# Turning the attention probabilities: one path for all query groups, a common column layout for the scores, and a later schedule

## The chip, the cores and the metric

The kernel runs on one core of a Trainium2 chip. The metric is the time of one execution in device microseconds; the median of three runs is given, and beside it one execution that the hardware profiler recorded. The core has five engines, each with its own queue of instructions that it works through in order: TensorE (PE, matrix products; its weight loads are shown as PEld), VectorE (DVE), ScalarE (ACT), GpSimd (POOL), and SyncE (SP), which here issues the weight transfers. Engines wait for one another through semaphores. Products are accumulated in PSUM, a memory of its own, which the kernel hands out in slots.

## The reference

A sequence of 256 tokens of width 2048 goes through two layers in float32. The first is a Mamba-2 mixer. The second is sliding-window attention with 32 query heads in 4 groups; each group of 8 heads shares one key/value head of width 64. The window is 128, and each head has a sink that enters the softmax's denominator. Cut to the attention part:

```python
proj = x @ w_in
q    = rope(proj[..., :2048] + q_bias)        # (b, s, 4 groups, 8 heads, 64)
gate = proj[..., 2048:]
s = einsum("bcqhrd,bckhd->bchrqk", q_blocks, k_prev_and_own) * 64 ** -0.5
s = where((0 <= q - k) & (q - k < 128) & (k >= 0), s, -inf)
m = maximum(max(s), sink)
p = exp(s - m);  p = p / (sum(p) + exp(sink - m))
o = einsum("bchrqk,bckhd->bcqhrd", p, v_prev_and_own)
h = (o * silu(gate)) @ w_out
x = layernorm(ALPHA * x + h)
```

The 256 queries are two halves of 128 (`h` in the kernel). The first half sees only its own 128 keys under a causal mask. In the second half each query sees the last 128 keys, so a block of 64 queries touches 192 key columns: 64 that are cut by the window's far edge, 64 that are seen in full, and 64 that are cut by the diagonal.

## The kernel before

All large products are done to float32 accuracy with three matmuls: ACT copies the rounded high part of a weight (`wh`, L163), DVE subtracts to get the low part (`wl`, L166), and PE adds high·high, high·low and low·high. Weights come in units of 128x2048, as two transfers of 512 KB each on SP's queue (L154) into six raw buffers; the split runs two units ahead of the products.

The Mamba layer, its output and the shared keys and values fill about the first 685 us. Then comes the attention layer, whose stream of products is written out in `B_ORDER`: for each of the four groups `j` a query projection `q`, a gate projection `g` and an output projection `o`, four weight units each. After every unit `tick()` runs the small jobs whose count has come down to zero; `later(n, fn)` books a job `n` units ahead. The small jobs stand in the engines' queues at the place where they are run, apart from a scheduler that may move DVE, ACT and POOL instructions that are not pinned with `keep_in_program_order`. The jobs of one group are:

- `q_block`: four units of products (L975), then DVE adds the bias and rotates the first 16 columns of each head (rope, L957 to L965). One unit later `qtr` turns the queries: PE transposes (L1061), ACT copies them out of PSUM with the scale (L1065).
- `attend(j, 0)`, two units after the projection, and `attend(j, 1)`, three units after that (one for the last group): PE computes the scores (L1114 for the first half, L1121 for the second). For the second half the two blocks of 64 queries have their 192 columns at different places of the tile, and DVE selects the masked pieces with copies under a predicate on 64 rows each (L1137), after ACT copied the 128 columns in the middle (L1134). DVE takes the maximum (L1145), ACT the exponentials (L1151), DVE normalises (L1157).
- Turning the probabilities, so that keys lie on partitions. For all but one case this is `turn_far`: DVE turns 32x32 blocks (L1170), ACT moves the blocks of 32x256 to their places (L1179: 10 copies for the first half, 16 for the second), and for the second half DVE then multiplies two full copies with masks (L1186, 128x1024). The last group's second half uses `turn_p`: eight PE transposes (L1199) and four DVE multiplications by masks out of PSUM (L1205).
- `pv`: PE multiplies by the values (L1231 for the first half; L1245 and L1252 for the second), DVE multiplies by the gate out of PSUM into `o` (L1219), and ACT and DVE split the result (L1259, L1260) for the output projection. `o` shares its two buffers (tag `qt`) with the rotated queries. The PVs of both halves stand next to one another.
- `o` units: products L322 to L324, added to the residual stream by DVE (L329).

The scores, the query and key transposes, `turn_p` and the PVs share one pool of four PSUM slots (`ax`); the projections use another of four (`mm`). Beside all this the first layer's normalised rows get their gain and offset (`residual`, L1028 and L1029) in eight pieces spread over units 2 to 15, with the gain and offset rows fetched by four pairs of transfers on POOL's queue (`load_affine`, L1023) as the buffers come free. The keys are turned by `ktr` (L1012), two units after their projection, after a copy on POOL (L1007).

Of the kernel before, what the change touches and what calls it, by code (L numbers as in the profile page):

```python
# [83 lines left out]
def trunk(ctx: ExitStack, tc: tile.TileContext, A: dict, out: bass.AP, dbg=None):  # L84
# [31 lines left out]

    tri, anti = cc[:, 256:384], cc[:, 640:768]
    mask_a0 = cc[:, 768:896]
# [137 lines left out]

    def later(n, fn):
        pending.append([n, fn])

# [693 lines left out]
    def rope(v, h, n):  # L953

        c = cs[:, h : h + 1, :].to_broadcast([P, n, 8])
        s = sn[:, h : h + 1, :].to_broadcast([P, n, 8])
        t = bp.tile([P, 4, 8, 8], F32, tag="rt", name=nm("rt"), bufs=1)  # L957
        x1, x2 = v[:, :, 0:8], v[:, :, 8:16]
        a, b, d, e = [t[:, i, :n, :] for i in range(4)]
        nc.vector.tensor_tensor(a, x1, c, ALU.mult)  # L960
        nc.vector.tensor_tensor(b, x2, s, ALU.mult)
        nc.vector.tensor_tensor(d, x2, c, ALU.mult)
        nc.vector.tensor_tensor(e, x1, s, ALU.mult)
        nc.vector.tensor_tensor(x1, a, b, ALU.subtract)
        nc.vector.tensor_tensor(x2, d, e, ALU.add)  # L965

    def x_stat(ps, h, u, ui, pin=False, last=None):
# [3 lines left out]
        for k, i in todo:  # L971
# [7 lines left out]
            pinned(m, pin)  # L979


    kT = bp.tile([P, 4, S], F32, tag="kT", name="kT")
# [3 lines left out]
    for h in range(2):  # L986
        ps = mm_tile()
        for ui in range(4):
            if h == 0:

                kv_u.append(next_unit(ui == 1))
                if ui == 0:
                    center(1, *scale1)
            x_stat(ps, h, kv_u[ui], ui, h == 0, ((1, 1, 2, None), (1, None, None, None))[h][ui])
            if h == 0:
                for c in ((), (), (0, 1, 2, 3), ())[ui]:
                    if c % 2 == 0:
                        wide = bp.tile([P, 1024], F32, tag=("pt0", "pri")[c // 2], name=nm("x1"), bufs=1)
                    turn_x1(1, c, wide[:, c % 2 * 512 : c % 2 * 512 + 512])
        kd = bp.tile([P, 4, 2, 64], F32, tag="qt", name=nm("kd"), bufs=2)  # L1000
        nc.vector.tensor_tensor(
# [14 lines left out]

        later(2, ktr)

    def load_affine(c):

        for i, n in enumerate(("lng", "lnb")):
            gb1[i] = bp.tile([P, 512], F32, tag=f"gb{i}", name=nm("gb1"), bufs=1)
            nc.gpsimd.dma_start(gb1[i][:], A[n][0, c * 512 : (c + 1) * 512].partition_broadcast(P))  # L1023

    def residual(c, h):

        v = xr[:, h, c * 512 : (c + 1) * 512]
        tc.keep_in_program_order(nc.vector.tensor_tensor(v, v, gb1[0][:], ALU.mult))  # L1028
        nc.vector.tensor_tensor(v, v, gb1[1][:], ALU.add)  # L1029

    gb1 = {}
    load_affine(0)
    for c in range(4):
        if c:
            later(GB_AT[c], lambda c=c: load_affine(c))
        for h in range(2):
            later(RES_AT[2 * c + h], lambda c=c, h=h: residual(c, h))

    qT = {}
    sg = {}  # L1040
    os_ = {}
    firsts = []

    def q_block(j):
# [7 lines left out]
        for h in range(2):  # L1052
# [16 lines left out]

            later(1, qtr)  # L1070

# [13 lines left out]

    def first_pt():

        if not firsts:
            t = bp.tile([P, 4, 8, 32], F32, tag="pt0", name="pt0", bufs=1)
            for c in range(1, 4):  # L1090
                nc.gpsimd.memset(t[32 * c : 32 * c + 32, :c].rearrange("p c r a -> p (c r a)"), 0.0)
            firsts.append(t)
        return firsts[0]

    def attend(j, h):
# [3 lines left out]
        p = bp.tile([P, 1024], F32, tag="p", name=nm("p"), bufs=3)  # L1099
        far = j < 3 or h == 0  # L1100
        byhead = p[:].rearrange("p (c r b) -> p r c b" if far else "p (r c b) -> p r c b", r=8, c=4)
        per = 512 // nk
# [4 lines left out]
        for b in range(0, 4, per):  # L1107
            pss = [ax_tile(), ax_tile()]
            for i in range(per):
                for part in range(h + 1):  # L1110
                    for par in range(2):
# [7 lines left out]

                        qs, at = slice(64 * part, 64 * part + 64), i * nk + 64 * (1 - part)  # L1120
                        nc.tensor.matmul(  # L1121
# [3 lines left out]
            for par in range(2):  # L1125
# [7 lines left out]

                nc.scalar.copy(v, blocks(got[:, :, 64:192]))  # L1134
                for part, m, at in ((0, mask_own, 192), (1, mask_a0[:, 64:], 0)):
                    qs = slice(64 * part, 64 * part + 64)
                    nc.vector.copy_predicated(  # L1137
                        v[qs, :, 2 * part : 2 * part + 2, :],
                        blocks(m[qs].bitcast(U32).unsqueeze(1)).to_broadcast([64, per, 2, 32]),
                        blocks(got[qs, :, at : at + 64]),  # L1140
                    )
        sk = snk[:, j * 8 : j * 8 + 8]
# [17 lines left out]

        pts = {}

        def masked(kc, v):
            m = (anti, tri)[kc].rearrange("p (c b) -> p c b", b=32)
            return m.unsqueeze(1).to_broadcast([P, v, 4, 32])

        def turn_far():

            z = bp.tile([P, 4, 256], F32, tag="p", name=nm("z"), bufs=3)
            nc.vector.transpose(z[:].rearrange("p c f -> p (c f)"), p[:])  # L1170
            if h == 0:
                pts[0] = first_pt()
            else:
                for kc in range(2):
                    pts[kc] = bp.tile([P, 4, 8, 32], F32, tag=("pri", "own")[kc], name=nm("pt"), bufs=1)

            def moved(c):
                for i in range(c * (h == 0), 4):
                    nc.scalar.copy(  # L1179
                        pts[0][32 * c : 32 * c + 32, i].rearrange("p r a -> p (r a)"), z[32 * i : 32 * i + 32, c]  # L1180
                    )

            def parts():
                t, own = (pts[kc][:].rearrange("p c r b -> p r c b") for kc in range(2))
                for kc, d in ((1, own), (0, t)):
                    nc.vector.tensor_tensor(d, t, masked(kc, 8), ALU.mult)  # L1186

            for c in range(4):
                later(MOVE_AT[c], lambda c=c: moved(c))
            if h:  # L1190
                later(MASK_AT, parts)

        def turn_p():
            for kc in range(2):
                pts[kc] = bp.tile([P, 4, 8, 32], F32, tag=("pri", "own")[kc], name=nm("pt"), bufs=1)
            for par in range(2):
                pt = ax_tile()
                for a in range(4):
                    nc.tensor.transpose(  # L1199
                        pt[:, a * P : (a + 1) * P], p[:, (par * 4 + a) * P : (par * 4 + a + 1) * P], ident  # L1200
                    )
                got = blocks(pt[:].rearrange("p (a q) -> p a q", a=4))
                for kc in range(2):
                    t = pts[kc][:].rearrange("p c r b -> p r c b")[:, par * 4 : par * 4 + 4]
                    nc.vector.tensor_tensor(t, got, masked(kc, 4), ALU.mult)  # L1205

        def pv():
# [15 lines left out]

            def pt_of(kc, par, rows, c0, c1):
                return pts[kc][rows, c0:c1, par * 4 : par * 4 + 4, :].rearrange("p c a b -> p c (a b)")

# [9 lines left out]
            else:  # L1236
# [6 lines left out]
                for part in range(2):  # L1243
                    for par in range(2):
                        nc.tensor.matmul(  # L1245
                            into(part, par), vt[:, part, vs], pt_of(part, par, whole, 2 * part, 2 * part + 2),
                            start=True, stop=False,
                        )
                for par in range(2):
                    for part in range(2):  # L1250
                        rows = slice(64 * part, 64 * part + 64)
                        nc.tensor.matmul(  # L1252
                            into(part, par), vt[rows, 1 - part, vs],
                            pt_of(1 - part, par, rows, 2 * part, 2 * part + 2), start=False, stop=True,
                        )
# [6 lines left out]

        if far:
            turn_far()
        else:
# [39 lines left out]
    def centre(h, nb):  # L1305
        tag, n = ("p", 3) if h and nb in (0, 3) else (("pt0", "pri", "own", "pri")[nb], 1)
        t = bp.tile([P, 1024], F32, tag=tag, name=nm("t"), bufs=n)
# [67 lines left out]
def _layout(inputs):  # L1375
# [63 lines left out]
    cc[:, 512:640] = tri  # L1439
    cc[:, 640:768] = 1.0 - tri  # L1440
    cc[:, 896:1024] = np.tril(np.ones((P, P)))
    cc[:, 768:896] = np.where(i[None, :] <= i[:, None], 0.0, NEG)
# [22 lines left out]
```

## Time and profile before

| | |
|---|---|
| median of three runs | 991.89 us (991.82 to 992.39) |
| profiled execution, its own time | 992.29 us |
| its span in the trace | 990.3 us |
| PE busy | 979.4 us |
| DVE, ACT, POOL busy | 781.1, 599.4, 103.5 us |
| granted TensorE clock | 0.999 |

The span is what the trace shows from the first to the last instruction; 2.0 us lie around it. In the views, "busy" is the time in which an engine worked on instructions; PE's matmuls are pipelined, so their durations overlap, and the distance from one start to the next is what a matmul takes of the queue. A line of a timeline gives start, length, engine, source line, operation, output and inputs with their shape, how many instructions of the kind stand in the row, and in brackets the idle time before them with what ended it. In the list of waits a row names who waited, for whom, the total, the number of times and the longest.

### The profile page before, as it was taken

The page shows a single profiled execution, that of the slowest core. Times are in us where ns is not written, and L with a number is a line of the kernel's source. Part 1 is how long each engine was busy: PE and PEld are TensorE (multiplying, and loading weights), DVE is VectorE, ACT ScalarE, POOL GpSimd, SP SyncE. Part 2 cuts the span into 40 slices and gives each one's busy share as a digit, 9 for nine tenths or more (in the row PEclk, how much of TensorE's full clock was granted, in tenths as well). Part 3 has the DMA queues.
Part 4 walks back from the last instruction along what each step waited for, and adds up shares of the span by engine and source line. Part 5 has one row for each costly group of instructions (what it writes and reads, how often), then busy time and mean ns, then how long its engine had stood idle before and what let it go on. Part 6 is the DMA issues. An engine that isn't in the chain of part 4 may idle for free.

```text
span 990.3 us, 18070 instructions
## 1 busy us (share of the span) xinstructions
PE 979.4 (99%) x7076; PEld 892.2 (90%) x7076; DVE 781.1 (79%) x1211; ACT 599.4 (61%) x1076; POOL 103.5 (10%) x133
## 2 busy tenths in 40 slices
PE   9999999999999999999999999999999999999998
PEld 8999989999999998999999999888898888988976
DVE  7888896867786887686787687889678878687796
ACT  7585866547646654664664664566477575674652
POOL 0001303004003002100300300302000000000003
PEclk9999999999999999999999999999999999999999
DMA  9788577575576666656657466456755557547532
GB/s 362 254 278 310 170 262 220 173 236 171 194 235 187 217 209 195 202 186 209 202 175 237 141 205 213 152 178 217 236 169 175 164 160 239 151 152 219 184 108 85
DMA packets 61557, 198.89 MB, mean 201 GB/s; under 512 B 6849, under 2 KB 11361, under 8 KB 61217
## 3 DMA queue, kind: packets, MB, share of 16 engines
q1 hardware_dynamic: 58528, 188.53, 58.9%
q0 software_dynamic: 2336, 8.69, 2.9%
q8 instruction: 55, 0.90, 0.4%
q10 hardware_dynamic: 608, 0.52, 0.2%
q14 instruction: 30, 0.24, 0.1%
HBM read 195.49 MB, written 2.23 MB: 200 GB/s over the span
## 4 chain that ended last, share of the span: by engine, by line
PE 92%; DVE 4%; ACT 2%; issue 1%; DVEq 0%; ACTq 0%
PE mm L251 50%; PE mm L975 9%; PE mm L322 9%; PE mm L323 8%; PE mm L324 8%; PE ax L630 2%; DVE wl L166 1%; ACT p L1151 1%; PE ax L606 1%; ACT pt L1179 0%; PE mm L389 0%; PE ax L589 0%; ACT wh L163 0%; PE ax L906 0%; PE ax L1114 0%
## 5 line engine op out<-in xcount | busy, mean ns | idle before, releaser
L166 DVE TENSOR_TENSOR wl<-wr,wh 128x1024 fp32r<-128x1024 f32 (+2 forms) x338 | 393.5, 1184 | 99.9 <-ACT wh L163 96.5
L163 ACT ACTIVATE wh<-wr 128x1024 fp32r<-128x1024 f32 (+2 forms) x338 | 331.2, 1010 | 154.8 <-issue 51.4
L251 PE MATMUL mm<-xH,wh 128*128 128x256 f32 x1280 | 356.1, 278 | 0.0
L251 PE MATMUL mm<-xL,wh 128*128 128x256 f32 x1280 | 354.6, 277 | 0.0
L251 PE MATMUL mm<-xH,wl 128*128 128x256 f32 x1280 | 354.5, 277 | 0.0
L251 PEld LDWEIGHTS mm<-xH,wh 128*128 128x128 f32 x1280 | 240.8, 188 | 2.0 <-issue 0.5
L251 PEld LDWEIGHTS mm<-xL,wh 128*128 128x128 f32 x1280 | 240.7, 188 | 1.0
L251 PEld LDWEIGHTS mm<-xH,wl 128*128 128x128 f32 x1280 | 240.5, 188 | 0.0
L322 PE MATMUL mm<-wh,yH 128*128 128x512 f32 x256 | 101.5, 397 | 0.0
L323 PE MATMUL mm<-wh,yL 128*128 128x512 f32 x256 | 99.9, 390 | 0.0
L324 PE MATMUL mm<-wl,yH 128*128 128x512 f32 x256 | 99.9, 390 | 0.0
L646 POOL TENSOR_TENSOR yz<-yz,z 128x256 f32<-128x256 f32 x32 | 32.5, 1024 | 468.6 <-DVE yz L641 468.6
L251 PE MATMUL mm<-x1H,wh 128*128 128x256 f32 x256 | 71.9, 281 | 0.0
L493 DVE SCALAR_TENSOR_TENSOR cv<-mm,pc,cv 128x255 f32<-128x255 f32 x144 | 68.7, 477 | 3.3 <-ACT cv L491 1.9
L251 PE MATMUL mm<-x1H,wl 128*128 128x256 f32 x256 | 71.1, 278 | 0.0
L251 PE MATMUL mm<-x1L,wh 128*128 128x256 f32 x256 | 71.1, 278 | 0.0
L975 PE MATMUL mm<-wh,x1H 128*128 128x512 f32 x160 | 63.0, 394 | 0.0
L975 PE MATMUL mm<-wl,x1H 128*128 128x512 f32 x160 | 61.9, 390 | 0.0
L975 PE MATMUL mm<-wh,x1L 128*128 128x512 f32 x160 | 60.9, 390 | 0.0
L322 PEld LDWEIGHTS mm<-wh,yH 128*128 128x128 f32 x256 | 48.1, 188 | 10.3 <-DVE z L582 0.9
L324 PEld LDWEIGHTS mm<-wl,yH 128*128 128x128 f32 x256 | 48.1, 188 | 10.1
L331 DVE SCALAR_TENSOR_TENSOR xr<-mm,r,xr 128x512 f32<-128x512 f32 x64 | 47.1, 745 | 11.7 <-PE mm L324 7.4
(226 smaller groups left out, 1373.1 us busy)
## 6 DMA issues: line engine op xcount, KB each, us to landing
wr<-in_wa SPq DMA_DIRECT2D x154, 512.0 KB, 5.1
wr<-in_wo SPq DMA_DIRECT2D x64, 512.0 KB, 4.5
wr<-in_wq SPq DMA_DIRECT2D x32, 512.0 KB, 4.0
wr<-in_wg SPq DMA_DIRECT2D x31, 512.0 KB, 4.9
wr<-in_wb SPq DMA_DIRECT2D x16, 512.0 KB, 4.7
wr<-in_wb SPq DMA_DIRECT2D x32, 256.0 KB, 3.7
rb<-rscr SPq DMA_DIRECT2D x11, 512.0 KB, 4.1
wr<-in_wkv SPq DMA_DIRECT2D x8, 512.0 KB, 5.0
```

The lines of the kernel that those rows point to most:

```text
L163: m = nc.scalar.activation(h[:, sl], v, AF.Copy)
L166: m = nc.vector.tensor_tensor(l[:, sl], v, h[:, sl].bitcast(F32), ALU.subtract)
L251: m = nc.tensor.matmul(ps, a, b, start=first and i == 0, stop=last and i == 2)
L322: pinned(nc.tensor.matmul(ps, aH[:, k, hs], u.h[:, ks], start=k == 0 and add is None, stop=False), pin)
L323: pinned(nc.tensor.matmul(ps, aL[:, k, hs], u.h[:, ks], start=False, stop=False), pin)
L324: pinned(nc.tensor.matmul(ps, aH[:, k, hs], u.l[:, ks], start=False, stop=k == 3), pin)
L331: nc.vector.scalar_tensor_tensor(v, ps, rms[:, h : h + 1], v, ALU.mult, ALU.add)
L493: nc.vector.scalar_tensor_tensor(a[:, sft:], ps[:, : S - sft], w(3 - sft), a[:, sft:], ALU.mult, ALU.add)
L606: nc.tensor.transpose(ps[:, o : o + P], st.xs[i][:, c * P : (c + 1) * P], ident)
L630: nc.tensor.matmul(ps[64 * r : 64 * r + 64, cols], xd[:, c, r, :], e[:, 256:] if c else e[:, :256], start=c == 0, stop=c == 1,)
L646: nc.gpsimd.tensor_tensor(v, v, st.z[i][:], ALU.mult)
L975: m = nc.tensor.matmul(ps[:], (x1H, x1L, x1H)[i][:, kk, hs], (u.h, u.h, u.l)[i][:, ks], start=(kk, i) == (0, 0), stop=ui == 3 and (k, i) = ...
```

## The change

Every second half, the last group's too, is turned by the DVE block transpose and ACT copies; `turn_p` is gone. Both 64-query blocks of the second half now write their 192 score columns from the same column on: 128 columns that ACT copies, and 64 behind them of which DVE selects the diagonal part with one copy under a predicate for all 128 rows. In this layout a query's two partly masked pieces share 64 columns. After the block transpose these are masked by DVE ahead of the copies, with two 64-column masks: one product goes to a small tile `ze`, one stays in `z`. ACT then moves 20 blocks per second half into two tiles that are kept for all groups, `ptw` (128x1024, 14 blocks) and `pte` (128x512, 6 blocks), whose other blocks POOL once set to zero.

The schedule changes with it. `B_ORDER` puts the third query projection ahead of the first output projection, and the fourth ahead of the second. Query transposes come two units after their projection instead of one, the first half's scores three instead of two, the second half's always three after the first's, key transposes three instead of two. The PVs of the two halves are booked separately (`PV_AT`), and come one to four units apart, save for the last group's, which come in neighbouring units. All eight residual pieces are done in units 2 to 6, and all gain and offset rows are fetched early, into four pairs of rows. The last operation of the rotation is pinned in program order. The mask constants are replaced accordingly.

```diff
-B_ORDER = [("q", 0), ("g", 0), ("q", 1), ("g", 1), ("o", 0), ("q", 2), ("g", 2), ("o", 1),
-           ("q", 3), ("g", 3), ("o", 2), ("o", 3)]
-RES_AT = [2, 3, 6, 7, 11, 12, 14, 15]
-MOVE_AT, MASK_AT = [2, 2, 3, 3], 4
-PV_AT = [[8, 5], [5, 4]]
-GB_AT = [0, 4, 8, 13]
+B_ORDER = [("q", 0), ("g", 0), ("q", 1), ("g", 1), ("q", 2), ("o", 0), ("g", 2), ("q", 3),
+           ("o", 1), ("g", 3), ("o", 2), ("o", 3)]
+MOVE_AT = [[2, 3, 3, 4], [3, 4, 5, 6]]
+MOVE_LAST = [2, 3, 3, 4]
+PV_AT = [[6, 7], [6, 7], [8, 7], [7, 5]]
+RES_AT = [2, 2, 3, 3, 4, 5, 5, 6]
...
-        nc.vector.tensor_tensor(x2, d, e, ALU.add)
+        tc.keep_in_program_order(nc.vector.tensor_tensor(x2, d, e, ALU.add))
...
+    def load_affine(c):
+
+        if c:
+            t = bp.tile([P, 1024], F32, tag="pt0" if c == 1 else "p", name=nm("gb1"), bufs=1 if c == 1 else 3)
+            gb1[c] = t[:, :512], t[:, 512:]
+        else:
+            gb1[c] = [bp.tile([P, 512], F32, tag=f"gb{i}", name=nm("gb1"), bufs=1)[:] for i in range(2)]
+        for v, n in zip(gb1[c], ("lng", "lnb")):
+            nc.gpsimd.dma_start(v, A[n][0, c * 512 : (c + 1) * 512].partition_broadcast(P))
...
-        later(2, ktr)
+        later(3, ktr)
+    for c in range(1, 4):
+        load_affine(c)
+    for i, n in enumerate(RES_AT):
+        later(n, lambda i=i: residual(i // 2, i % 2))
...
-            later(1, qtr)
+            later(2, qtr)
...
-                        qs, at = slice(64 * part, 64 * part + 64), i * nk + 64 * (1 - part)
+                        qs, at = slice(64 * part, 64 * part + 64), i * nk
...
-                nc.scalar.copy(v, blocks(got[:, :, 64:192]))
-                for part, m, at in ((0, mask_own, 192), (1, mask_a0[:, 64:], 0)):
-                    ...
+                nc.scalar.copy(v, blocks(got[:, :, :128]))
+                nc.vector.copy_predicated(
+                    v[:, :, :2, :],
+                    blocks(mask_own.bitcast(U32).unsqueeze(1)).to_broadcast([P, per, 2, 32]),
+                    blocks(got[:, :, 128:192]),
+                )
...
+            if h:
+                e = bp.tile([P, 2, 8, 32], F32, tag="ze", name=nm("ze"), bufs=1)
+                for d, m in ((e, mask_e), (z, mask_w)):
+                    m = m.rearrange("p (c b) -> p c b", b=32).unsqueeze(2).to_broadcast([P, 2, 8, 32])
+                    nc.vector.tensor_tensor(d[:, :2], z[:, :2], m, ALU.mult)
...
                 for i in range(c * (h == 0), 4):
-                    nc.scalar.copy(
-                        pts[0][32 * c : 32 * c + 32, i].rearrange("p r a -> p (r a)"), z[32 * i : 32 * i + 32, c]
-                    )
+                    if h == 0:
+                        move(still[0][:, i], z, i, c)
+                        continue
+                    at = c ^ (2 * (i // 2))
+                    if (c, i) not in ((0, 1), (3, 2)):
+                        move(still[1][:, i], z, i, at)
+                    if at < 2 and (c, i) not in ((1, 0), (2, 3)):
+                        move(still[2][:, i % 2], e, i, at)
...
-        def turn_p():
-            ...
-        if far:
-            turn_far()
-        else:
-            later(3, turn_p)
-        later(PV_AT[j == 3][h], pv)
+        turn_far()
+        later(PV_AT[j][h], pv)
         if h == 0:
-            later(1 if j == 3 else 3, lambda: attend(j, 1))
+            later(3, lambda: attend(j, 1))
...
-            later(2, lambda j=j: attend(j, 0))
+            later(3, lambda j=j: attend(j, 0))
```

More of the change, by code (lines that the diff above doesn't have):

```diff
@@ L255, in trunk, with later @@
     pending = []
-    def later(n, fn):
-        pending.append([n, fn])
+    def later(n, fn, place=None):
+        pending.insert(len(pending) if place is None else place, [n, fn])
     def tick():
@@ L1041, in trunk @@
     os_ = {}
-    firsts = []
+    still = []
     def q_block(j):
@@ L1084, in gate_block @@
             )
[L1086 to L1093, printed above, removed]
     def attend(j, h):
@@ L1193, in turn_p @@
-        def turn_p():
[L1194 to L1205, printed above, removed]
+            z = bp.tile([P, 4, 8, 32], F32, tag="p", name=nm("z"), bufs=3)
@@ new lines, in turn_far @@
+            nc.vector.transpose(z[:].rearrange("p c r b -> p (c r b)"), p[:])
+            if not still:
+                still.append(bp.tile([P, 4, 8, 32], F32, tag="pt0", name="pt0", bufs=1))
+                for c in range(1, 4):
+                    nc.gpsimd.memset(still[0][32 * c : 32 * c + 32, :c].rearrange("p c r a -> p (c r a)"), 0.0)
+            if h and not still[1:]:
+                still.append(bp.tile([P, 4, 8, 32], F32, tag="pri", name="ptw", bufs=1))
+                still.append(bp.tile([P, 2, 8, 32], F32, tag="own", name="pte", bufs=1))
+                for t, c, i in ((1, 0, 1), (1, 3, 2), (2, 1, 0), (2, 2, 1)):
+                    nc.gpsimd.memset(still[t][32 * c : 32 * c + 32, i].rearrange("p r a -> p (r a)"), 0.0)
@@ L1207, in pv @@
+            for c in range(4):
+                later((MOVE_LAST if j == 3 else MOVE_AT[h])[c], lambda c=c: moved(c))
         def pv():
@@ L1253, in pv @@
                             into(part, par), vt[rows, 1 - part, vs],
-                            pt_of(1 - part, par, rows, 2 * part, 2 * part + 2), start=False, stop=True,
+                            pt_of(2, par, rows, 0, 2), start=False, stop=True,
                         )
@@ L1305, in centre @@
     def centre(h, nb):
[L1306 removed]
+        tag, n = ("p", 3) if h and nb in (0, 3) else (("pt0", "pri", "pt0", "pri")[nb], 1)
         t = bp.tile([P, 1024], F32, tag=tag, name=nm("t"), bufs=n)
@@ L1439, in _layout @@
     cc[:, 512:640] = tri
-    cc[:, 640:768] = 1.0 - tri
-    cc[:, 896:1024] = np.tril(np.ones((P, P)))
+    for g in range(4):
+        at, own = slice(32 * g, 32 * g + 32), np.zeros((32, 64))
+        own[:, g % 2 * 32 : g % 2 * 32 + 32] = tri[:32, :32]
+        if g % 2:
+            own[:, :32] = 1.0
+        cc[at, 640:704] = own if g > 1 else 1.0 - own
+        cc[at, 704:768] = 1.0 - own if g > 1 else own
+    cc[:, 896:960] = np.tril(np.ones((64, 64)))[i % 64]
     cc[:, 768:896] = np.where(i[None, :] <= i[:, None], 0.0, NEG)
```

63 lines of the change are left out of this document (18 added, 45 removed).

## The prediction

> **What bounds the kernel now.** I read the page's first parts, then TensorE's waits, its timeline around each of those waits, and a table by stage.
>
> ```profile
> PE 979.4 (99%) x7076; PEld 892.2 (90%) x7076; DVE 781.1 (79%) x1211; ACT 599.4 (61%) x1076; POOL 103.5 (10%) x133
> ...
> L163 ACT ACTIVATE wh<-wr 128x1024 fp32r<-128x1024 f32 (+2 forms) x338 | 331.2, 1010 | 154.8 <-issue 51.4
> ```
>
> PE is busy for 979.4 us of a span of 990.3. The 10.9 us between are all that the schedule can still give, beside PE work that is taken away. (The second row, a split of weights on ACT, is used below for its mean of 1010 ns.) The waits of PE name their places:
>
> ```profile
> PE ax L1061 <- DVE qt L965: 2.0, 1, 2.0
> PE ax L1199 <- DVE p L1157: 1.7, 1, 1.7
> PE ax L1114 <- DVE o L1219: 1.3, 1, 1.3
> ```
>
> The columns are total, count and longest. All three, 5.0 us, lie in the attention layer, where the change acts. PE's timeline shows each wait; a block that was not held up stands ahead of the first and of the second (713.61 and 720.04):
>
> ```profile
> 713.61 1.04 PE L1061 MATMUL ax<-cc,qt 128*128 128x128 f32 x8
> 714.40 0.36 PE L251 MATMUL mm<-x1H,wh 128*128 128x256 f32 x1
> ...
> 761.13 0.60 PE L1061 MATMUL ax<-cc,qt 128*128 128x128 f32 x4
> 763.77 0.63 PE L1061 MATMUL ax<-cc,qt 128*128 128x128 f32 x4 [2.04 <-DVE qt L965]
> 764.15 0.37 PE L251 MATMUL mm<-x1H,wh 128*128 128x256 f32 x1
> ```
> ```profile
> 719.84 0.28 PE L251 MATMUL mm<-x1H,wl 128*128 128x256 f32 x1
> 720.04 1.16 PE L1114 MATMUL ax<-kT,qT 64*128 64x128 f32 x16
> 721.13 0.39 PE L251 MATMUL mm<-x1H,wh 128*128 128x256 f32 x1
> 721.36 0.28 PE L251 MATMUL mm<-x1L,wh 128*128 128x256 f32 x1
> 721.47 0.28 PE L251 MATMUL mm<-x1H,wl 128*128 128x256 f32 x1
> ...
> 772.26 0.49 PE L1114 MATMUL ax<-kT,qT 64*128 64x128 f32 x2
> 774.02 1.16 PE L1114 MATMUL ax<-kT,qT 64*128 64x128 f32 x14 [1.28 <-DVE o L1219]
> 775.11 0.39 PE L251 MATMUL mm<-x1H,wh 128*128 128x256 f32 x1
> ```
> ```profile
> 942.56 0.39 PE L323 MATMUL mm<-wh,oL 128*128 128x512 f32 x1
> 942.79 0.39 PE L324 MATMUL mm<-wl,oH 128*128 128x512 f32 x1
> 944.90 1.06 PE L1199 MATMUL ax<-cc,p 128*128 128x128 f32 x8 [1.73 <-DVE p L1157]
> 945.72 0.48 PE L322 MATMUL mm<-wh,oH 128*128 128x512 f32 x1
> 946.04 0.39 PE L323 MATMUL mm<-wh,oL 128*128 128x512 f32 x1
> ```
>
> Since matmuls overlap, I price by the distance between starts, not by durations: a block costs from its first start to the start of what follows. The windows show who is short of time there (columns: stretch, its length, then busy time of PE, weight load, DVE, ACT, POOL, clock, DMA share, GB/s):
>
> ```profile
> 665.00:675.00 10.00, 10.00 (x54) 8.54 (x53) 9.63 (x19) 8.89 (x23) 0.00 (x0) 1.00 0.74 211
> 695.00:705.00 10.00, 10.00 (x50) 8.36 (x49) 4.69 (x7) 5.17 (x8) 1.07 (x2) 1.00 0.78 262
> 755.00:777.00 22.00, 18.69 (x160) 16.45 (x159) 21.93 (x40) 15.75 (x30) 1.61 (x3) 1.00 0.75 233
> 932.00:955.00 23.00, 21.27 (x108) 16.18 (x107) 21.28 (x37) 17.29 (x39) 1.06 (x2) 1.00 0.68 229
> ```
>
> DVE is full for all of 755 to 777 and nearly so in 932 to 955. These are the stretches with the waits, and everywhere between them PE ran without a hole. So what counts is whether DVE's queue delivers in time at the three places, and whether something else becomes late.
>
> **The change part by part.**
>
> Query transposes (L1061) run two units after their projection instead of one. A unit is 24 products of 0.228 us on PE, 5.46 us (942.56 to 942.79 is one such step, rounded; times of the schedule below are counted in units). The rotation that they waited for gets 5.46 us more, and was 2.04 us late. At j=1 the block took 764.15 − 761.13 = 3.02 us against 714.40 − 713.61 = 0.79. Gain **2.23**.
>
> Scores of query group 1, first half (L1114 at 772.26): two matmuls, then a wait for the DVE operation that empties a PSUM slot of the attention pool (`o`, L1219), because both probability-times-value products (PV) of group 0 stood directly ahead of them. Afterwards the two halves' PVs of group 0 come at units 13 and 17 and these scores at unit 15. The first half's `o` shares its buffers with the query tiles, so it is emptied only behind the transposes at unit 14, still one unit ahead of the scores. The block took 775.11 − 772.26 = 2.85 against 721.13 − 720.04 = 1.09. Gain **1.76**.
>
> The last turn (L1199) leaves PE. The wait ahead of it, 944.90 − 942.79 = 2.11 less the usual step of 0.23, is 1.88; the eight transposes take 945.72 − 944.90 = 0.82; the slower resumption, 0.32 against 0.23, is 0.09. Gain **2.79**, if what replaces it is in time for PV. That is a chain of a DVE transpose, two masks and 20 ACT copies. These rows, of DVE, ACT and PE, price it; the first three of PE are the last group's PVs:
>
> ```profile
> 951.37 1.08 PE L1231 MATMUL ax<-pt,vt 128*64 128x512 f32 x4
> 952.27 1.03 PE L1245 MATMUL ax<-pt,vt 128*64 128x256 f32 x8
> ...
> 953.83 0.50 PE L322 MATMUL mm<-wh,oH 128*128 128x512 f32 x1
> ```
> ```profile
> 797.30 2.48 DVE L1137 COPY_PREDICATED p<-cc,ax 64x128 f32<-64x128 uint32 x8
> ...
> L1205 DVE TENSOR_TENSOR pt<-ax,cc x4: 686/689/690, 948.1 to 949.9; 128x512 f32<-128x512 f32 x4
> ...
> L1179 ACT COPY pt<-z x88: 400/404/410, 734.1 to 936.6; 32x256 f32<-32x256 f32 x88
> ...
> 791.69 1.53 PE L1121 MATMUL ax<-kT,qT 64*64 64x192 f32 x32
> 793.15 0.51 PE L322 MATMUL mm<-wh,oH 128*128 128x512 f32 x1
> ...
> 756.07 6.65 ACT L1179 COPY pt<-z 32x256 f32<-32x256 f32 x16 [0.18 <-DVE z L1170]
> ...
> 810.39 6.64 ACT L1179 COPY pt<-z 32x256 f32<-32x256 f32 x16 [0.85 <-DVE z L1170]
> ```
>
> For group 1 the scores start at 791.69 and the turned array is there just ahead of 810.39, 18.7 us later. Two masks on 128x512 add 2 × 0.69, 20 copies 20 × 0.415 = 8.3 (spacing 6.64/16), and four predicated copies fewer take off 4 × 0.31 = 1.2: 27.2 us. PV comes five units after the scores in the last group: 27.3, the scores themselves 793.15 − 791.69 = 1.46, and the first half's PV between, 952.27 − 951.37 = 0.9 with its break of 0.2: 29.9. Slack 2.7 us, and 1.7 with a split (1.01) among the copies. The last turn is covered; without that cover it is a wait of PE at 1 to 1.
>
> By the Trainium skill, page "VectorE: DVE Perf Modes", section "Rules for kernel authors", a 128×128 transpose belongs on TensorE when a PSUM destination is fine: the opposite of this part. By it the last turn would stay on PE, the gain would be the wait alone, and the sum 0.9 smaller (987.0). The trace speaks against it here: the 0.91 us that go lie on a queue that is 99% busy, the 9.7 us of masks and copies that come lie on engines with 21% and 39% free.
>
> The other turns: ACT copies go from 88 to 120 (32 × 0.404 = 12.9 us), DVE gets less to do: eight masks of 128x512 take the place of six twice as wide and four as wide, and 16 predicated copies of 32 go. ACT has 390 us free over the span, so I cost this at nothing if the order on its queue holds. That is the tightest place: in the changed ACT queue the query copy of group 1 (L1065, between transposes and scores) stands behind all 20 copies of group 0's second half. In the old trace that half's turn was done just ahead of 756.07; one unit later is 761.5, with 20 copies 769.8, with one split 770.8, and the copy is done some 0.7 later, 771.5. The scores stood at 772.26; without the stall of 2.23, a unit of 5.46 later, and with the second half's PV (953.83 − 952.27 = 1.56) no longer ahead of them, they come at about 774.0. Slack **2.5 us**, an estimate; at group 2 the order is the same, with DVE less full.
>
> PSUM: scores of a second half take all four slots of the pool. Group 1's come one unit after the PV that fills the last of group 0's `o`: 5.46 less that PV's 1.56 leaves its emptying 3.9 us; group 2's is no tighter.
>
> Residual (L1028/L1029) and its affine rows: 16 DVE operations in units 2 to 6 instead of 2 to 15, so ten more there, 6.9 us at the 0.69 of the nearest row of that size. DVE has 5.3 us free at 695 to 705 alone, a third of those units. The affine DMAs that come earlier on POOL's queue, 256 KB each, stand ahead of the key copies (L1007):
>
> ```profile
> 678.77 1.33 POOL L1007 COPY kd<-kd 128x256 f32<-128x256 f32 x1 [2.08 <-DVE kd L965]
> ...
> gb<-in_lnb POOLq DMA_DIRECT2D x4, 256.0 KB, 5.1
> ```
>
> They land in 5.1 us; the key transposes that follow these copies get a unit more. The DMA engines have 26% free in 665 to 675. Four memsets join POOL, 10% busy. Nothing of it on the path: between 0 and +1 (one split late); I take 0.
>
> What costs: each time attention work breaks into the product stream PE loses a little on leaving (719.84 to 720.04 is 0.20, where 721.36 to 721.47 is the usual 0.11) and on coming back (721.13 to 721.36 is 0.23): 0.20. Afterwards there are five more breaks, four for PVs taken apart and one for the scores that no longer follow a PV: **+1.0**. The bounds are 0 and, with the 0.09 + 0.09 more of L322's resumption (793.15), 1.5.
>
> Sum: −2.23 − 1.76 − 2.79 + 1.0 = **−5.8 us**. Against the profiled execution, 992.29 us with a span of 990.3, that is 986.5. The median of the runs is 991.89, 0.40 under that execution, so I predict **986.1**.
>
> **Rivals.**
>
> *Slower: the query copy comes late.* ACT's longer row of copies stands ahead of L1065, and DVE, full at 755 to 777, feeds it. Up to 2.5 us late costs nothing; each us beyond is a us on PE, at groups 1, 2 and 3. The change is undone at 2.5 + 5.8 = 8.3 us in one place, or about 4.4 in each of three; 6 us late in each gives 986.1 + 3 × 3.5 = 996.6. For it: all 20 copies come first. Against: the residual leaves DVE just there. 0.07.
>
> *The waits only move.* With DVE late by more than a unit, L1061 and L1114 still wait, 3.99 us, and only 2.79 − 1.0 comes out: 990.1. Against: one unit is over twice either wait. 0.08.
>
> *PSUM slots.* The pool stays at four. The Trainium skill, page "Perfetto Trace Analysis", section "Optimization Strategy", says that consistent bubbles can mean too little SBUF or PSUM for the next tile; the wait of 1.28 us on `o` agrees, but stands at one place only. In rows: that wait comes back at two places, 2.6 us: 988.7; at three, 990.0. 0.16, together with a late query copy or last turn of 1 to 4 us.
>
> *Breaks are free:* 985.1; any better has 0.03.
>
> **How the numbers follow.** The forecast, 985.0 to 987.5, has 0.66. Within 0.2% (2.0 us, about what a measurement of this kernel can tell from no change) lie the moved waits, 0.08; slower is 0.07; the returning PSUM wait and a small lateness, 987.5 to 989.9, count as faster. Faster 0.85. The range 985.0 to 989.8 leaves out 0.18.
>
> **What would show it.** PE's list of waits without L1061, without the turn on PE, and without L1114. PE busy lower by about 0.8 − 1, so nearly equal; the idle 10.9 us down to about 5. If I am wrong, PE waits for ACT `qT` L1065 (first rival), for DVE `o` at the second half's scores (PSUM), for ACT's copies at the last PV, or for a split near 700 (residual).

## The result, and the profile after

The changed kernel takes **987.34 us** (median of six, 986.98 to 987.8), the kernel before, run beside it, 992.21 (six, 991.82 to 992.39). The ratio is 0.9948, with a 95% interval of 0.9938 to 0.9959: faster by 4.9 us, where 5.8 had been predicted. The span of the profiled execution went from 990.3 to 985.6 us.

The first lines of the page after, with the engines' busy time, and the whole list of PE's waits:

```profile
span 985.6 us, 18078 instructions
...
PE 979.8 (99%) x7068; PEld 890.7 (90%) x7068; DVE 773.8 (79%) x1194; ACT 611.9 (62%) x1108; POOL 103.3 (10%) x137
```
```profile
PE ax L372 <- DVE zero L360: 1.0, 1, 1.0
```

All three waits of the attention layer are gone; the one that is left stands at the start of the kernel, as it did before. PE is busy for no less time, though eight matmuls are gone, which is a first sign that something else on PE grew. (Source lines are one to fifteen or so higher or lower than before: transposes of queries are L1066, scores L1109 and L1116, PVs L1219, L1233 and L1240, products of the gate projection L252, the others L976 and L323 to L325. DVE's multiplication by the gate, L1219 before, is L1207, and L1219 is now a PV on PE.)

The windows after, same stretches and columns as before:

```profile
755.00:777.00 22.00, 22.00 (x187) 20.64 (x186) 17.82 (x33) 18.40 (x36) 0.54 (x1) 1.00 0.63 190
932.00:955.00 23.00, 23.00 (x109) 17.23 (x108) 18.23 (x23) 18.90 (x34) 0.00 (x0) 1.00 0.64 224
695.00:705.00 10.00, 10.00 (x49) 8.35 (x49) 7.43 (x12) 5.18 (x8) 1.56 (x3) 1.00 0.62 211
```

PE runs through both stretches. DVE, full before, has 4.2 and 4.8 us free; ACT carries 2.7 and 1.6 us more. At 695 to 705 DVE took the residual pieces, 2.7 us more, and still has 2.6 free.

The two tight places come out looser than worked out. These rows are of ACT's and PE's timelines after:

```profile
770.78 0.58 ACT L1070 ACTIVATE qT<-ax 128x512 f32<-128x512 f32 x1
...
943.18 0.40 ACT L1177 COPY pte<-ze 32x256 f32<-32x256 f32 x1
```
```profile
774.66 1.16 PE L1109 MATMUL ax<-kT,qT 64*128 64x128 f32 x16
775.76 0.39 PE L252 MATMUL mm<-x1H,wh 128*128 128x256 f32 x1
...
947.59 1.08 PE L1233 MATMUL ax<-ptw,vt 128*64 128x256 f32 x8
```

The query copy of group 1 ends at 771.36 and the scores that read it start at 774.66: 3.3 us. The last group's last copy ends at 943.58 and its PV starts at 947.59: 4.0 us.

### The profile page after: what moved, and what is told of

It reads as the page before. It is cut to its first block, busy times and chain, and to the rows that moved or that the text cites. A ratio compares the mean times of both kernels' runs of the same rounds, so it can differ in the third digit from the quotient of the medians.

```text
span 985.6 us, 18078 instructions
## 1 busy us (share of the span) xinstructions
PE 979.8 (99%) x7068; PEld 890.7 (90%) x7068; DVE 773.8 (79%) x1194; ACT 611.9 (62%) x1108; POOL 103.3 (10%) x137
## 3 DMA queue, kind: packets, MB, share of 16 engines
HBM read 195.49 MB, written 2.23 MB: 201 GB/s over the span
## 4 chain that ended last, share of the span: by engine, by line
PE 99%; DVE 0%; DVEq 0%; issue 0%
PE mm L252 54%; PE mm L976 11%; PE mm L323 9%; PE mm L324 9%; PE mm L325 9%; PE ax L631 2%; PE ax L607 1%; PE ax L1116 1%; PE ax L1109 0%; PE ax L590 0%; PE mm L390 0%; PE ax L1233 0%; PE ax L1219 0%; PE ax L1066 0%; PE ax L907 0%; PE ax L372 0%
## 5 line engine op out<-in xcount | busy, mean ns | idle before, releaser
L252 PE MATMUL mm<-xH,wh 128*128 128x256 f32 x1280 | 355.4, 278 | 0.0
L252 PE MATMUL mm<-xL,wh 128*128 128x256 f32 x1280 | 354.1, 277 | 0.0
L252 PE MATMUL mm<-xH,wl 128*128 128x256 f32 x1280 | 353.9, 276 | 0.0
L252 PEld LDWEIGHTS mm<-xH,wh 128*128 128x128 f32 x1280 | 240.7, 188 | 1.8 <-issue 0.5
L252 PEld LDWEIGHTS mm<-xL,wh 128*128 128x128 f32 x1280 | 240.6, 188 | 1.0
L252 PEld LDWEIGHTS mm<-xH,wl 128*128 128x128 f32 x1280 | 240.5, 188 | 0.0
L323 PE MATMUL mm<-wh,yH 128*128 128x512 f32 x256 | 101.4, 396 | 0.0
L325 PE MATMUL mm<-wl,yH 128*128 128x512 f32 x256 | 99.7, 389 | 0.0
L252 PE MATMUL mm<-x1H,wh 128*128 128x256 f32 x256 | 71.9, 281 | 0.0
L252 PE MATMUL mm<-x1L,wh 128*128 128x256 f32 x256 | 71.1, 278 | 0.0
L252 PE MATMUL mm<-x1H,wl 128*128 128x256 f32 x256 | 71.0, 278 | 0.0
L976 PE MATMUL mm<-wh,x1H 128*128 128x512 f32 x160 | 63.1, 394 | 0.0
L976 PE MATMUL mm<-wl,x1H 128*128 128x512 f32 x160 | 61.8, 389 | 0.0
L976 PE MATMUL mm<-wh,x1L 128*128 128x512 f32 x160 | 60.9, 390 | 0.0
L323 PEld LDWEIGHTS mm<-wh,yH 128*128 128x128 f32 x256 | 48.1, 188 | 10.3 <-DVE z L583 1.0
L325 PEld LDWEIGHTS mm<-wl,yH 128*128 128x128 f32 x256 | 48.1, 188 | 10.2
```

Source lines behind the costliest of these rows:

```text
L252: m = nc.tensor.matmul(ps, a, b, start=first and i == 0, stop=last and i == 2)
L323: pinned(nc.tensor.matmul(ps, aH[:, k, hs], u.h[:, ks], start=k == 0 and add is None, stop=False), pin)
L325: pinned(nc.tensor.matmul(ps, aH[:, k, hs], u.l[:, ks], start=False, stop=k == 3), pin)
L976: m = nc.tensor.matmul(ps[:], (x1H, x1L, x1H)[i][:, kk, hs], (u.h, u.h, u.l)[i][:, ks], start=(kk, i) == (0, 0), stop=ui == 3 and (k, i) = ...
```

## Experiments

The part of the program ahead of the attention layer varies from one execution to the next: the first gate product stands at 708.1 us in one profile of a kernel and at 709.4 in another of the same kernel. So besides the medians I compare the **attention stretch** of each trace, from the first gate product to the start of the last PE block of the kernel. For before and after its ends are these rows:

```profile
708.15 0.28 PE L251 MATMUL mm<-x1H,wh 128*128 128x256 f32 x1
...
983.57 1.99 PE L1342 MATMUL ax<-t,dg 128*128 128x256 f32 x6
```
```profile
708.19 0.28 PE L252 MATMUL mm<-x1H,wh 128*128 128x256 f32 x1
...
978.95 1.99 PE L1327 MATMUL ax<-t,dg 128*128 128x256 f32 x6
```

That is 275.42 us before and 270.76 after, 4.66 less: all of the 4.6 us between the two spans. A second profile of the changed kernel gives 270.76 again, and two profiles of another kernel 268.96 and 268.97. The column of differences below is against the changed kernel, 270.76, except where it says otherwise. The medians come from five groups of runs; the kernel before, run in each of them, had medians of 992.21 to 992.92, so medians of different groups differ by some tenths without any edit.

| kernel | median, us | attention stretch, us | difference | PE's waits in it |
|---|---|---|---|---|
| before | 992.21 | 275.42 | +4.66 | 2.0, 1.3, 1.7 |
| changed | 987.34 | 270.76 | | none |
| transposes one unit after | 987.56 | 270.20 | −0.56 | none |
| residual spread | 987.68 | 270.76 | 0.00 | none |
| both | 988.08 | 270.94 | +0.18 | 0.6 |
| transposes one unit after, no PV ahead of them | 987.79 | 270.65 | +1.69 to PVs together | 1.7 |
| the same, residual spread | 988.30 | 271.41 | +2.45 to PVs together | 2.4 |
| before, with the last turn off PE | 995.76 | 276.67 | +1.25 to before | 3.6, 2.1, 1.3 |
| PVs together | 986.11, 986.00 | 268.96, 268.97 | −1.80 | none |
| PVs directly ahead of scores | 987.26 | 269.97 | −0.79 | none |
| the same, residual spread | 986.85 | 270.44 | −0.32 | none listed |
| copies twice | 996.49 | 279.00 | +8.24 | 3.2, 2.7, 1.6 |

### Which part took away the wait on the rotation

Query transposes one unit after their projection, alone:

```diff
-            later(2, qtr)
+            later(1, qtr)
```

> The changed kernel with the query transposes one unit after their projection again; everything else stays. My theory, that the unit more is what removed the wait on the rotation: PE waits 2.0 us for DVE before the transposes of group 1 again, about 989.3 us. Rival, that the wait went because DVE's queue no longer holds the residual pieces, the wide masks and their like at that place: in the changed kernel's trace the second rotation ended at 762.76 us and the earlier place of its transposes is some 762.9, so the wait is under 0.5 us and the time is 987.0 to 987.8.

The residual pieces as before, alone:

```diff
-RES_AT = [2, 2, 3, 3, 4, 5, 5, 6]
+RES_AT = [2, 3, 6, 7, 11, 12, 14, 15]
+GB_AT = [0, 4, 8, 13]
...
-    for c in range(1, 4):
-        load_affine(c)
-    for i, n in enumerate(RES_AT):
-        later(n, lambda i=i: residual(i // 2, i % 2))
+    for c in range(4):
+        if c:
+            later(GB_AT[c], lambda c=c: load_affine(c))
+        for h in range(2):
+            later(RES_AT[2 * c + h], lambda c=c, h=h: residual(c, h))
```

> The changed kernel with the eight residual pieces at units 2 to 15 and the gain and offset rows fetched at four times, as before. My theory: the transposes keep their unit more, so no wait of PE comes back; at most the query copy of group 1, 3.3 us ahead of its scores in the changed kernel, comes later, and the time stays within 0.5 us of 987.3. Rival, that the residual was what kept DVE late: a wait of PE of 1 to 2 us near 768 to 775 us, 988.3 to 989.3.

And both edits at once:

> The changed kernel with both undone: transposes one unit after the projection, residual spread over units 2 to 15. If either change alone is enough to remove the wait, it comes back only here, about 2 us at group 1: 989.3 us. If it was the unit more alone, this run is as slow as the one with the early transposes and the early residual. If neither is the cause (the masks on half the columns, done ahead of the copies, relieve DVE), no wait comes back here either and the time stays at 987.0 to 987.8.

The medians were 987.56, 987.68 and 988.08 us. No wait came back with either edit alone, and 0.6 us with both, not the 2 us of before. With the early transposes the stretch even became 0.56 shorter, since three of the four transposes then follow a PV directly and share its break, and since two slow units fewer stand in it (see the last section; 0.4 us). That hid what I was after: at group 1 a PV of the first half stood directly ahead of the transposes and gave DVE another microsecond. So I ran the early transposes again with the PVs elsewhere, by the edit of the PVs together below, with the early residual and with the spread one.

> The changed kernel with the query transposes one unit after the projection and the PVs of a group together, so that no PV stands ahead of the transposes of group 1. The early transposes alone showed no wait, but a PV of 1.01 us stood ahead of them. Theory now: that PV covered the lateness of the rotation; without it PE waits about 0.9 us before the second four transposes. Rival, that DVE is early enough by itself: no wait.

> As the run just named, with the residual pieces spread over units 2 to 15 besides. If the lateness of 2.0 us before came from the residual pieces in DVE's queue in part, and the rest was hidden by the PV: PE waits 1.6 to 1.8 us here, against 0.9 with the early residual. If the residual plays no part, both runs wait the same.

PE's timeline of the first of them, and then of the second:

```profile
763.27 0.60 PE L1066 MATMUL ax<-cc,qt 128*128 128x128 f32 x4
764.81 0.63 PE L1066 MATMUL ax<-cc,qt 128*128 128x128 f32 x4 [0.94 <-DVE qt L966]
...
815.94 0.63 PE L1066 MATMUL ax<-cc,qt 128*128 128x128 f32 x4 [0.73 <-DVE qt L966]
```
```profile
762.30 0.60 PE L1064 MATMUL ax<-cc,qt 128*128 128x128 f32 x4
764.60 0.63 PE L1064 MATMUL ax<-cc,qt 128*128 128x128 f32 x4 [1.70 <-DVE qt L967]
...
815.73 0.63 PE L1064 MATMUL ax<-cc,qt 128*128 128x128 f32 x4 [0.73 <-DVE qt L967]
```

At group 1 the wait is 0.94 us with the early residual and 1.70 with the spread one, as expected, and there is a wait of 0.73 at group 2 that the kernel before did not have. Against the kernel with the PVs together the stretch is longer by 1.69 and 2.45 us, which is the sum of the waits each time. Moving the PV did not move the rotation: with the early residual its last operation ends 54.4 us after the first gate product, with the PV ahead and without it. So the unit more removes the wait by itself (residual spread: none, and a stretch of 270.76 to the hundredth). Moving the residual takes 0.76 us off it, and a PV that happens to stand ahead hides another microsecond. The common column layout, the new masks and the pin on the rotation stand in all of these runs; what each of them does by itself was not tested.

### The scores behind the PVs

Both PVs of group 0 directly ahead of the first half's scores of group 1 again, in unit 15:

```diff
-PV_AT = [[6, 7], [6, 7], [8, 7], [7, 5]]
+PV_AT = [[8, 5], [6, 7], [8, 7], [7, 5]]
...
-                later((MOVE_LAST if j == 3 else MOVE_AT[h])[c], lambda c=c: moved(c))
+                later((MOVE_LAST if j in (0, 3) else MOVE_AT[h])[c], lambda c=c: moved(c))
```

> The changed kernel with both PVs of group 0 directly ahead of the first half's scores of group 1, at unit 15, as they stood before (the copies of that half run two units earlier). My theory for the wait of 1.28 us on the emptying of PSUM: it needs only this neighbourhood and comes back with 1 to 1.8 us, less 0.56 for the breaks saved, 987.8 to 988.6. Rival, that it was DVE's lateness in that stretch: no wait over 0.3 us, 986.8.

The same with the residual spread:

> The changed kernel with both PVs of group 0 directly ahead of the scores of group 1, and the residual spread as before. The neighbourhood alone brought no wait: DVE emptied the PSUM slot 0.2 us after its PV had ended. Theory now, that before it was the residual in DVE's queue (two pairs of it stood between the PV and the emptying) together with the neighbourhood: the wait comes back, 1.0 to 1.8 us. Rival, that the DVE work saved elsewhere is enough: no wait over 0.3 us.

Here my theory fell, twice. First PE's and DVE's rows of before, then those of the run with this edit alone, then PE's of the run with the residual spread:

```profile
769.79 1.08 PE L1231 MATMUL ax<-pt,vt 128*64 128x512 f32 x4
770.70 0.60 PE L1245 MATMUL ax<-pt,vt 128*64 128x256 f32 x4
```
```profile
770.82 1.22 DVE L166 TENSOR_TENSOR wl<-wr,wh 128x1024 fp32r<-128x1024 f32 x1
771.95 0.69 DVE L1028 TENSOR_TENSOR xr<-xr,gb 128x512 f32<-128x512 f32 x1
772.67 0.69 DVE L1029 TENSOR_TENSOR xr<-xr,gb 128x512 f32<-128x512 f32 x1
773.28 0.68 DVE L1219 TENSOR_TENSOR o<-ax,sg 128x512 f32<-128x512 f32 x1
```
```profile
776.02 1.03 PE L1233 MATMUL ax<-ptw,vt 128*64 128x256 f32 x8
```
```profile
774.93 1.23 DVE L167 TENSOR_TENSOR wl<-wr,wh 128x1024 fp32r<-128x1024 f32 x1 [0.26 <-ACT wh L164]
776.24 0.69 DVE L1207 TENSOR_TENSOR o<-ax,sg 128x512 f32<-128x512 f32 x1
```
```profile
775.91 1.45 PE L1107 MATMUL ax<-kT,qT 64*128 64x128 f32 x16
777.29 0.39 PE L253 MATMUL mm<-x1H,wh 128*128 128x256 f32 x1
```

Before, the first half's PV had given way to the second's on PE at 770.70, and DVE began to empty its slot at 773.28, 2.6 us later, behind a split and two residual operations. With the neighbourhood restored DVE began at 776.24, 0.2 us after PE had gone on at 776.02, and PE did not wait. With the residual spread as well, the scores' block took 777.29 − 775.91 = 1.38 us instead of 1.09: 0.3 us, not 1.3. So standing directly behind the PVs was not enough for the wait; DVE had to be late, and neither this neighbourhood nor the residual nor both bring that lateness back here. In these runs the place lies one unit later than it did before. Whether the rest is due to that unit, or to the wide masks that stood in DVE's queue ahead of it before, was not separated.

### The last turn off PE, without the new order

The kernel before, with one edit:

```diff
-        far = j < 3 or h == 0
+        far = True
```

> The kernel before with its own schedule, but the last group's second half turned by DVE and ACT like the others. If taking the eight transposes off PE is a gain in itself: 0.8 us of PE work and 1.9 us of waiting go, 989.4 us. My theory, that the turn off PE needs the later PV, which the new order of projections gives: normalised at 944.8, turned at 946, sixteen copies to 952.6, two wide masks to 955, while PE is at the second half's PV at 949.5; PE waits 5.5 to 7.5 us there, 995 to 997 us.

995.76 us, against 992.92 for the kernel before beside it (ratio 1.003, 1.0019 to 1.0042). PE's timeline in the last group:

```profile
950.68 1.08 PE L1231 MATMUL ax<-pt,vt 128*64 128x512 f32 x4
951.69 0.50 PE L322 MATMUL mm<-wh,oH 128*128 128x512 f32 x1
...
958.51 1.08 PE L1245 MATMUL ax<-pt,vt 128*64 128x256 f32 x8 [3.58 <-DVE pt L1186]
```

The second half's PV came 6.8 us after the first's had ended, within the 5.5 to 7.5 expected. But that was expected as a wait, and PE did not stand for all of it: 13 products (3.0 us at 0.228) came in between, and the wait was 3.6. The stretch is 1.25 longer than before: −2.79 for the turn, +3.9 for what the 13 products do not cover, and a break. The median is 2.8 us higher, and so within the 995 to 997 expected, but 1.6 us of that lie outside the stretch: in the profiled execution the first gate product stands at 710.2 us instead of 708.1, behind code that was not edited. What delays it there was not found, so it is in part luck that the median met its range. What the run shows is that in the old schedule, with the old masks, the turn off PE gains nothing. In the new schedule the last second half's PV comes five units after its scores instead of four, and the turn is covered. Whether a later PV in the old order would do as well was not tried. The Trainium skill's rule (page "VectorE: DVE Perf Modes", section "Rules for kernel authors", the 128×128 transpose on TensorE) is borne out by this run in the old schedule (1.25 us longer), and not by the changed kernel, where the longer way is covered with 4.0 us to spare.

### PVs of a group together

```diff
-PV_AT = [[6, 7], [6, 7], [8, 7], [7, 5]]
+PV_AT = [[10, 7], [10, 7], [10, 7], [8, 5]]
```

> The changed kernel with the PVs of both halves of a group next to one another again, each pair in the unit of the second half. My reading of the two traces: a pair costs 0.91 + 0.96 + 0.59 us and one break, taken apart 1.01 + 1.01 + 0.59 and two breaks of 0.2, so 0.36 us more in each of four groups: 1.4 us less here, 985.9 us, and no wait of PE comes back. If breaks cost nothing: 987.3. Rival, that the distance between the PVs is needed for PSUM slots: PE waits at the second half's scores one unit later, over 0.5 us in each of two groups, 987 to 988.

> The changed kernel with the PVs of a group next to one another, once more beside the changed kernel itself. By the trace of the first run, 1.8 us less in the attention layer than the changed kernel: 1.44 of breaks and blocks, the rest from units of the gate projection that run at 118 ns a step instead of 113. If the slow units come and go by chance, the difference here lies between 1.2 and 2.0 us.

> The changed kernel unaltered, as the comparison for the run with the PVs together: 987.3 us if the first measurement stands, and four units of the gate projection at 118 ns a step if those belong to the program rather than to chance.

The first of these gave 986.11 us (six, 985.59 to 991.69, the second highest 987.32); the other two ran beside one another and gave 986.00 (five, 985.88 to 986.91) and 987.74 (five, 987.14 to 988.14). The stretch is 1.80 shorter both times, and no wait came back. It is the fastest version here. PE's timeline of the first half's PV after, and of the pair in this kernel:

```profile
761.25 0.28 PE L252 MATMUL mm<-x1H,wl 128*128 128x256 f32 x1
761.45 1.08 PE L1219 MATMUL ax<-pt,vt 128*64 128x512 f32 x4
762.46 0.39 PE L252 MATMUL mm<-x1H,wh 128*128 128x256 f32 x1
762.68 0.28 PE L252 MATMUL mm<-x1L,wh 128*128 128x256 f32 x1
```
```profile
785.40 1.08 PE L1219 MATMUL ax<-pt,vt 128*64 128x512 f32 x4
786.31 1.03 PE L1233 MATMUL ax<-ptw,vt 128*64 128x256 f32 x8
787.27 0.66 PE L1240 MATMUL ax<-pte,vt 64*64 64x256 f32 x8
787.86 0.50 PE L976 MATMUL mm<-wh,x1H 128*128 128x512 f32 x1
```

Alone, the first half's PV takes 762.46 − 761.45 = 1.01 us, in the pair 0.91; the second half's first block 1.01 against 0.96. With a break of 0.2 that is 0.36 a group, 1.4 in all. Three slow units fewer, told of below, take off nearly 0.6 more. About 0.2 comes back: in the last group the transposes now stand in two pieces, at 891.55 and 893.21, with five products between them, which is one more break.

### A dose of copies

```diff
                     if (c, i) not in ((0, 1), (3, 2)):
                         move(still[1][:, i], z, i, at)
+                        move(still[1][:, i], z, i, at)
```

> The changed kernel with every copy into the wide tile of a second half done twice: 14 copies more of 0.415 us, 5.8 us of ACT, in each of four groups. This doses the row of copies ahead of the query copy. By the distances in the changed kernel's trace (query copy done 771.4 and scores at 774.7 for group 1, 3.3 us; 3.8 at group 2; last copies done 943.6 and PV at 947.6, 4.0) PE waits 2.5, 2.0 and 1.8 us, about 993.6 us. If ACT's free time hides them all, 987.3. If my distances are too large because splits move behind the copies as well, over 996.

996.49 us, a stretch 8.24 longer, where 993.6 us had been expected; the time fell into the range of the third case, over 996. PE's timeline, at the rows with a wait:

```profile
776.55 1.16 PE L1109 MATMUL ax<-kT,qT 64*128 64x128 f32 x16 [1.53 <-ACT qT L1070]
...
829.04 1.16 PE L1109 MATMUL ax<-kT,qT 64*128 64x128 f32 x16 [1.66 <-ACT qT L1070]
...
893.28 0.50 PE L323 MATMUL mm<-wh,oH 128*128 128x512 f32 x1 [1.63 <-DVE qt L1060]
...
955.07 0.65 PE L1234 MATMUL ax<-ptw,vt 128*64 128x256 f32 x4 [1.91 <-ACT ptw L1177]
956.52 0.65 PE L1234 MATMUL ax<-ptw,vt 128*64 128x256 f32 x4 [0.79 <-ACT ptw L1177]
```

DVE's timeline ahead of the third of them:

```profile
889.06 1.23 DVE L167 TENSOR_TENSOR wl<-wr,wh 128x1024 fp32r<-128x1024 f32 x1 [3.02 <-ACT wh L164]
...
892.54 0.69 DVE L1060 TENSOR_TENSOR qt<-mm,bias 128x512 f32<-128x512 f32 x1
```

5.8 us more of copies in each group cost 1.5, 1.7 and 2.7 us at the three places named, 5.9 of the 6.3 expected; ACT's free time, 38% of the span in the changed kernel, did not hide them. A fourth place, a wait of 1.6 on the bias of the last queries, was not foreseen. There DVE had stood idle for 3.0 us until ACT gave it the high part of a weight, and so came late to the bias, which takes the last queries out of PSUM: weight splits on ACT had moved behind the longer row of copies, as the third case said. So the distances held, but they are not all that the copies delay. The other 0.7 us of the 8.24 were not traced. The distances read off the trace, 3.3 to 4.0 us, are what keeps the changed kernel fast, and they are short.

## Why the prediction was right, and where it was off

The direction, the three waits and the range (985.0 to 989.8) were right. The gain was 4.66 us in the attention stretch, 4.87 between medians, instead of 5.8. The signs named were there too: the three waits are off PE's list, its busy time is nearly equal (0.4 more), and its idle time fell from 10.9 to 5.8 us.

- **Query transposes, −2.23.** Gone. The reason given, the unit more, is enough by itself; the residual, which the prediction costed at nothing, would have taken off 0.76 of that wait.
- **Scores of group 1, −1.76.** Gone: the block took 775.76 − 774.66 = 1.10 us. The reason given, the PVs directly ahead, failed: that neighbourhood came back and the wait did not. What is shown is that DVE was 2.6 us late in emptying the slot before, and 0.2 us in the changed kernel with that neighbourhood restored. What freed DVE there stays open, so that this term came out to size is in part luck: taking the PVs apart was not needed for it, and the stretch is shorter with the pair of group 0 together again (0.79) and with all pairs together (1.80).
- **Last turn, −2.79.** Gone, and covered with 4.0 us to spare where 2.7 had been worked out. In the old schedule the move makes the kernel slower.
- **Tight places.** The query copy was placed at 771.5 and measured at 771.36; its scores at 774.0, and measured at 774.66: the first half's PV, now alone at 761.45, costs 0.3 more with its break, and two units ahead run slowly, 0.4. No wait, as said. That the slack is real was shown by the dose.
- **PSUM, residual, affine rows, POOL.** No wait of PE came from any of them. The residual spread again changes the stretch by nothing.
- **What costs, +1.0: the step that was mis-sized.** 6.78 of gains less 4.66 leaves 2.1 us, outside the bounds of 0 to 1.5. The five breaks at 0.2 were about right. Left out was that the blocks themselves take longer when they stand apart: 4 × (0.10 + 0.05) = 0.6 us. A further 0.4 us are two more slow units of the gate projection, below; both together with the breaks make 2.0. With it goes the statement that the idle 10.9 us are all that the schedule can give beside PE work taken away: these 2.1 us lie in PE's busy time, and the schedule made them.

Of the rivals none came true. The late query copy has its price shown by the dose, but from 3.3 us on, not 2.5.

## What to carry to other kernels

When the product engine is full, the price of a small block is more than its matmuls, since the break comes on top: here 0.2 us for leaving the stream and coming back, and 0.05 to 0.1 more for each block that stands alone. Work that waits for a late engine should be booked one unit later; work that does not should stand together. A move off the full engine paid here only where the consumer stood late enough for the length of the new way, so the order that gives this time belongs to the change, and the move alone may cost.

## What the runs showed of the hardware

After a break the stream of 128x256 products can stay slow for a whole unit of 48 products. After the query transposes of group 0, from PE's timeline after, and further on behind the scores:

```profile
720.58 0.28 PE L252 MATMUL mm<-x1H,wl 128*128 128x256 f32 x1
720.69 0.28 PE L252 MATMUL mm<-x1H,wh 128*128 128x256 f32 x1
720.81 0.28 PE L252 MATMUL mm<-x1L,wh 128*128 128x256 f32 x1
720.93 0.28 PE L252 MATMUL mm<-x1H,wl 128*128 128x256 f32 x1
...
727.63 0.28 PE L252 MATMUL mm<-x1H,wh 128*128 128x256 f32 x1
727.75 0.28 PE L252 MATMUL mm<-x1L,wh 128*128 128x256 f32 x1
727.86 0.28 PE L252 MATMUL mm<-x1H,wl 128*128 128x256 f32 x1
727.97 0.28 PE L252 MATMUL mm<-x1H,wh 128*128 128x256 f32 x1
```

The steps are 118 ns in the first unit and 113 in the second, with the same instruction and the clock at 1.00. The 118 hold to the end of the unit: 0.2 us for 48 products. Three of the four such units in the changed kernel end at a break; the one that starts at 846.37 is followed without a break by a unit at 113. Before, two units ran so; after, these four, in both profiles of that kernel; with the PVs together, one in both profiles. So it belongs to the program, not to chance. What sets it was not found.
